# Low weight parts by an accumulating DMA, used last, in a hybrid DeltaNet, Conformer and diffusion step

## The chip, the cores and the metric

The kernel runs on one core of a Trainium2 chip. The metric is the device time of one execution in microseconds (us); lower is better. Where several runs are given, their median and their lowest and highest time stand beside each other.

## What is computed

One trunk layer on 640 tokens: 128 context tokens and 512 latent tokens, in five chunks of 128. The reference in its core:

```python
h = rmsnorm(x, norm1) * (1 + sc1) + sh1          # adaLN modulation from c @ w_ada
p = h @ w_in                                     # 1024 -> 7200 columns
qkv, z, ab, glu, gates = jnp.split(p, SPLITS, axis=-1)
qkv = silu(dwconv_seq(qkv, conv_qkv))            # width 5
o, s_fin = bidir_delta(q, k, v, g, beta, s0)     # 8 heads, both directions, chunks of 64
y_a = (rmsnorm(o, norm_o) * silu(z)) @ w_a_out
u = dwconv(glu_a * sigmoid(glu_b)) + b_dw        # width 31
y_b = silu(layernorm(u, ln_g, ln_b)) @ w_b_out
x = x + g1 * ((sigmoid(ga) * y_a + sigmoid(gb) * y_b) @ w_o)
h2 = rmsnorm(x, norm2) * (1 + sc2) + sh2
x = x + g2 * ((silu(h2 @ wg) * (h2 @ wu)) @ w_down)
```

All of it is in fp32. The matmuls multiply in a format with a shorter mantissa (fp32r in the names of tiles). A product of a weight w and an activation x is therefore made of three matmuls: each factor is split into a high part, wh and xh, which that format holds, and the low part that is left, wl = w - wh and xl = x - xh. Their sum wh·xh + wh·xl + wl·xh collects in PSUM.

## The kernel before, in words

*Stages.* Up to about 45 us the inputs and the first w_ada tiles are loaded and h is built: hh (its high part) and hl (its low part), each 8 tiles of 128 features by 640 tokens. Stage 1, 45 to 770 us, makes the 56 projections of 128 columns with w_in (`proj_in`, L448), each followed by what its columns are for: `conv_silu` (L472) for q, k and v, gates for z and for the merge, the wide convolution; beside them run the DeltaNet's decay matrices, the inverses by blocks and the scans of eight heads. At its end come half of w_a_out (`first_half`, L906) and w_b_out (`conv_branch`, L912). From L1069 on, 770 us to the end, follow the rest of w_a_out, w_o, w_gu and w_down.

*A projection.* `proj` (L131) loops over the 8 tiles of 128 rows of the weights (kt), over the three products, and over the two halves of the tokens (256 and 384 columns, `HALVES`): 48 matmuls, called a unit here. For each kt the low part of the weights is needed directly behind its two high products.

*A weight tile.* `load_w` (L117) takes the next of four buffers in rotation (`NWR` = 4, `w_slots`), lets SyncE issue the load into it (wr, L121), lets ScalarE write the high part into one of two buffers wh (L107 of `split`), and an engine subtract (L108 of `split`): wl = wr - wh. wl is the same memory as wr, read as another type. `low["eng"]` says which engine subtracts: VectorE (V) from L115 on, GpSimd (G) from L1070 on; the first two loads, `pre[1024]` and `pre[0]` (L262, L266), name VectorE themselves. `ada_part` (L460) takes the next of the same four buffers for a tile of w_ada, 32 times, so that units and w_ada tiles then alternate, and uses it in 8 small matmuls (L468) behind the unit.

*What sets the order.* The program is written by a planner, a loop (L1060) over five generators (scans, inverses, preps, gather, mains), each of which gives out a piece of the work and a cost in us; the one with the lowest sum so far is next. The order on each engine is that of the program's text as the scheduler places it; each engine takes its instructions in order, and waits on semaphores for the others. The loads stand in SyncE's queue. GpSimd makes small work in stage 1: memsets of the convolution's edges (L477), inverse square roots by a power (L521), masks (L589), the row operations of the inverses (L603), casts (L655).

*The lines of the prediction.* L478, L481 and L485 are ScalarE's copies, first tap and tanh of `conv_silu`, L483 and L487 VectorE's other taps and the last product; L494 transposes the result on TensorE for the chunks of a head. L600, L603, L609, L611, L615 and L626 are the inverses; L714 to L764 the scan, in which L740 scales v by a decay and L744 is the matmul that updates the state. aux<-atd, tgd<-tb, tb<-tgd and og<-ogd are transfers to and from scratch tensors in DRAM (atd, tgd, ogd).

Of the kernel before, what the change touches and what calls it, by code (L numbers as in the profile page):

```python
# [9 lines left out]
F32 = mybir.dt.float32  # L10
# [4 lines left out]
AF = mybir.ActivationFunctionType  # L15
ALU = mybir.AluOpType
# [3 lines left out]
P = 128  # L20
# [35 lines left out]
def hybrid_step(ctx, tc, I, O):  # L56
    nc = tc.nc
    es = ctx.enter_context
    V, S_, G, PE = nc.vector, nc.scalar, nc.gpsimd, nc.tensor
# [40 lines left out]
    def g3(ap, a):  # L100
        return ap.rearrange("p (a b) -> p a b", a=a)
# [4 lines left out]
    def split(hi, lo, x, lo_eng=None):  # L106
        S_.activation(hi, x, AF.Identity)  # L107
        return (lo_eng or V).tensor_tensor(out=lo, in0=x, in1=hi.bitcast(F32), op=ALU.subtract)  # L108
# [3 lines left out]
                          mybir.DependencyInfo(mybir.DependencyClass.NoSync, mybir.DependencyReason.DATA),  # L112
                          reason="order")

    low = {"eng": V}  # L115

    def load_w(src, lo_eng=None, after=None, wh=None):  # L117
        a, b = src.shape[1], src.shape[2]
        n = a * b
        wr, wl = next(w_next)  # L120
        ld = nc.sync.dma_start(out=g3(wr[:, :n], a), in_=src)  # L121
        if after is not None:
            order(ld, after)
        wh = T_("wh", "wh", F32R) if wh is None else wh
        split(wh[:, :n], wl[:, :n], wr[:, :n], lo_eng or low["eng"])
        return g3(wh[:, :n], a), g3(wl[:, :n], a)

    def cols_of(w, c0, n=P):
# [2 lines left out]
    def proj(w, xh, xl, nk, pp=None, hfs=(0, 1), cut=HALVES, tiled=False, rows=P):  # L131
        pp = pp or mm_pair()
        wh, wl = w
        for kt in range(nk):
            for j, (a, b) in enumerate(((wh, xh), (wh, xl), (wl, xh))):
                for hf in hfs:
                    c = cut[hf]
                    out, x = pp[hf][:rows, :c.stop - c.start], b[kt // 4]
                    if tiled:
                        out, x = g3(out, (c.stop - c.start) // P), x[:, c.start // P:c.stop // P, kt % 4, :]  # L140
                    else:
                        x = x[:, kt % 4, c]
                    PE.matmul(out, a[:, kt, :], x,  # L143
                              start=(kt == 0 and j == 0), stop=(kt == nk - 1 and j == 2))
        return pp

    def halves(pp, ap, cut=HALVES):
# [20 lines left out]
    rows = T_("dd", "rows")[:, :P]  # L168
    G.memset(rows, 0.0)
    for k, (nm, n) in enumerate((("c_ctx", 8), ("c", 8), ("norm1", 8), ("norm2", 8))):  # L170
        src = I[nm] if nm == "c_ctx" else I[nm][0]
# [96 lines left out]
    for pr in range(4):  # L268
        ws = wada[pr]
        pa = sm_ps()  # L270
        for kk in range(NK):
            for g in range(4):
                j, k = g // 2, g % 2
# [6 lines left out]
        for k in range(2):  # L280
            kt = 2 * pr + k
# [4 lines left out]
            for r, (c0, n) in enumerate(SPANS):  # L286
                v, hi, lo = (t[kt // 4][:, kt % 4, c0:c0 + n] for t in (xT, hh, hl))
                b = modB[:, kt, r:r + 1]
# [1004 lines left out]
```

## Time and profile before

| what | value |
| --- | --- |
| median of 3 runs | 1344.68 us |
| lowest and highest | 1344.32 and 1345.86 us |
| the profiled execution | 1345.78 us, its span 1342.9 us |
| granted TensorE clock, mean | 0.985 of full speed |
| ScalarE busy | 503.2 us, 37% of the span |
| VectorE busy | 842.3 us, 63% of the span |
| GpSimd busy | 298.1 us, 22% of the span |
| DMA | 157.31 MB, mean 117 GB/s |

The span is the time between the first and the last instruction that the profiler saw; the execution's own time holds 2.9 us more. Busy shares are means over stages with different limits, so the prediction reads them by stage. In a row, L143 is line 143 of the kernel before, `mm<-hh,wl` is output and inputs by their names in the program, PE is TensorE, DVE VectorE, ACT ScalarE, POOL GpSimd and SP SyncE; PEld is TensorE's loading of stationary tiles, and a q behind a name (SPq) is the queue that issues an engine's DMAs.

### The profile page before, as it was taken

The page shows a single profiled execution, that of the slowest core. Times are in us where ns is not written, and L with a number is a line of the kernel's source. Part 1 is how long each engine was busy: PE and PEld are TensorE (multiplying, and loading weights), DVE is VectorE, ACT ScalarE, POOL GpSimd, SP SyncE. Part 2 cuts the span into 40 slices and gives each one's busy share as a digit, 9 for nine tenths or more (in the row PEclk, how much of TensorE's full clock was granted, in tenths as well). Part 3 has the DMA queues.
Part 4 walks back from the last instruction along what each step waited for, and adds up shares of the span by engine and source line. Part 5 has one row for each costly group of instructions (what it writes and reads, how often), then busy time and mean ns, then how long its engine had stood idle before and what let it go on. Part 6 is the DMA issues. An engine that isn't in the chain of part 4 may idle for free.

```text
span 1342.9 us, 23244 instructions
## 1 busy us (share of the span) xinstructions
PE 1280.9 (95%) x9180; PEld 1200.7 (89%) x9180; DVE 842.3 (63%) x1663; ACT 503.2 (37%) x1080; POOL 298.1 (22%) x305
## 2 busy tenths in 40 slices
PE   5987999997999999999988999999999999999997
PEld 4986998996998999999988998899988999889996
DVE  5677896999766899998686784621224212243136
ACT  4326655343454554525354233432211222112223
POOL 1203312220010312211010036433300333003304
PEclk9988998999999999999999999999999999999999
DMA  9312443443343453324455893122222222222222
GB/s 338 114 54 83 122 150 128 127 139 91 116 123 100 140 146 98 108 78 128 138 182 191 288 288 95 51 76 79 79 77 67 78 79 79 65 77 79 79 71 86
DMA packets 179293, 157.31 MB, mean 117 GB/s; under 512 B 8032, under 2 KB 150769, under 8 KB 179185
## 3 DMA queue, kind: packets, MB, share of 16 engines
q1 hardware_dynamic: 179185, 155.83, 37.4%
q8 instruction: 72, 1.18, 0.4%
q14 instruction: 36, 0.29, 0.1%
HBM read 131.80 MB, written 24.00 MB: 116 GB/s over the span
## 4 chain that ended last, share of the span: by engine, by line
PE 58%; DVE 7%; DMA 3%; issue 2%; ACT 2%; POOL 1%; SPq 0%; POOLq 0%; DVEq 0%; ACTq 0%
PE mm L143 36%; PE sm L1113 9%; PE mm L1113 4%; PE sm L143 1%; PE sm L734 1%; PE sm L758 1%; DVE wl L108 1%; DMA aux<-atd 1%; PE sm L1158 1%; DMA og<-ogd 1%; PE sm L661 1%; PE sm L744 1%; PE sm L714 1%; POOL x L1209 1%; PE sm L494 1%
## 5 line engine op out<-in xcount | busy, mean ns | idle before, releaser
L107 ACT ACTIVATE wh<-wr 128x1024 fp32r<-128x1024 f32 (+1 forms) x154 | 152.6, 992 | 460.8 <-PE mm L143 177.3
L143 PE MATMUL mm<-hh,wh 128*128 128x384 f32 (+1 forms) x896 | 220.2, 320 | 5.5 <-ACT ci L478 3.6
L143 PE MATMUL mm<-hl,wh 128*128 128x384 f32 (+1 forms) x896 | 217.9, 316 | 0.0
L143 PE MATMUL mm<-hh,wl 128*128 128x384 f32 (+1 forms) x896 | 214.9, 315 | 0.4 <-DVE wl L108 0.4
L108 POOL TENSOR_TENSOR wl<-wr,wh 128x1024 fp32r<-128x1024 f32 (+1 forms) x59 | 132.9, 2255 | 355.6 <-ACT wh L107 343.4
L108 DVE TENSOR_TENSOR wl<-wr,wh 128x1024 fp32r<-128x1024 f32 (+1 forms) x95 | 109.0, 1148 | 104.4 <-ACT wh L107 93.1
L143 PEld LDWEIGHTS mm<-hh,wh 128*128 128x128 f32 x896 | 162.1, 191 | 12.7 <-issue 4.7
L143 PEld LDWEIGHTS mm<-hl,wh 128*128 128x128 f32 x896 | 165.6, 191 | 0.1
L143 PEld LDWEIGHTS mm<-hh,wl 128*128 128x128 f32 x896 | 164.2, 190 | 1.2 <-DVE wl L108 0.9
L143 PE MATMUL mm<-h2h,wl 128*128 128x256 f32 (+1 forms) x672 | 155.5, 309 | 0.0
L143 PE MATMUL mm<-h2l,wh 128*128 128x256 f32 (+1 forms) x672 | 154.7, 308 | 0.0
L143 PE MATMUL mm<-h2h,wh 128*128 128x256 f32 (+1 forms) x672 | 154.6, 307 | 0.0
L1259 DVE TENSOR_TENSOR ft<-ft,mm 128x256 f32<-128x256 f32 (+1 forms) x42 | 18.6, 482 | 189.4 <-PE mm L143 189.3
L143 PEld LDWEIGHTS mm<-h2h,wh 128*128 128x128 f32 x672 | 123.5, 189 | 0.2
L143 PEld LDWEIGHTS mm<-h2h,wl 128*128 128x128 f32 x672 | 122.7, 189 | 0.0
L143 PEld LDWEIGHTS mm<-h2l,wh 128*128 128x128 f32 x672 | 122.1, 188 | 0.0
L483 DVE SCALAR_TENSOR_TENSOR acc<-ci,colA,acc 128x642 f32<-128x642 f32 x96 | 86.7, 905 | 7.1 <-ACT acc L481 6.1
L1113 PE MATMUL sm<-wh,fh 128*128 128x512 f32 x152 | 60.4, 397 | 0.0
L1113 PE MATMUL sm<-wl,fh 128*128 128x512 f32 x152 | 60.0, 395 | 0.0
L1113 PE MATMUL sm<-wh,fl 128*128 128x512 f32 x152 | 59.6, 392 | 0.0
L108 DVE TENSOR_TENSOR fl<-ft,fh 128x640 fp32r<-128x640 f32 x22 | 46.5, 2112 | 16.5 <-ACT fh L107 16.5
L609 DVE TENSOR_TENSOR stmp<-M,X 128x30 f32<-128x30 f32 (+14 forms) x120 | 43.7, 364 | 3.2 <-POOL X L603 1.8
(346 smaller groups left out, 2427.2 us busy)
## 6 DMA issues: line engine op xcount, KB each, us to landing
wr<-in_w_in SPq DMA_DIRECT2D x56, 512.0 KB
wr<-in_w_gu SPq DMA_DIRECT2D x44, 512.0 KB
wr<-in_w_ada SPq DMA_DIRECT2D x32, 512.0 KB
wr<-in_w_down SPq DMA_DIRECT2D x22, 512.0 KB
wada<-in_w_ada SPq DMA_DIRECT2D x8, 1024.0 KB
atd<-et SPq DMA_DIRECT2D x40, 128.0 KB
aux<-atd SPq DMA_DIRECT2D x40, 128.0 KB
tgd<-tgt SPq DMA_DIRECT2D x16, 320.0 KB
```

Of the source, the lines that this page charges most:

```text
L107: S_.activation(hi, x, AF.Identity)
L108: return (lo_eng or V).tensor_tensor(out=lo, in0=x, in1=hi.bitcast(F32), op=ALU.subtract)
L143: PE.matmul(out, a[:, kt, :], x, start=(kt == 0 and j == 0), stop=(kt == nk - 1 and j == 2))
L483: V.scalar_tensor_tensor(out=acc[:, :n], in0=ci[:, k:k + n], scalar=vA[:, k, ct:ct + 1], in1=acc[:, :n], op0=ALU.mult, op1=ALU.add)
L494: PE.transpose(pt[:, c, :], src(c0 + c), ident)
L609: V.tensor_tensor(out=t, in0=bc(M[:, j + 1:, j:j + 1], [P, n, j]), in1=bc(X[:, j:j + 1, 0:j], [P, n, j]), op=ALU.mult)
L661: PE.matmul(pt[:, j, :], lhs[j], rhs[j], start=True, stop=True)
L714: PE.matmul(pr[:, d, j, :], TT[j].kT[:, ck[d], :], S[:, d, j, :], start=True, stop=True)
L734: PE.matmul(pv[:, d, j, :], Y1[:, d, j, ck[d], :], rhs, start=True, stop=True)
L744: PE.matmul(pS[:, d, j, :], TT[j].ktok[:, ck[d], :], vw[:, d, j, :], start=True, stop=True)
L1113: PE.matmul(acc[i], a[kt // 4][:, kt % 4, c], b[:, k2, :], start=(kt == 0 and j == 0), stop=(kt == nk - 1 and j == 2))
L1259: V.tensor_tensor(out=d, in0=d, in1=s, op=ALU.mult)
```

## The change

70 loads of weights in stage 1 are concerned: 54 tiles of 128x1024 (512 KB each) of w_in, and 16 of 128x512 (256 KB each) of w_a_out and w_b_out. For these, the low part is no longer subtracted by VectorE. ScalarE writes wh as before, then a second pass writes -wh over the loaded tile (wl and wr are one memory), and GpSimd issues a DMA that reads the same weights from DRAM again and adds them to what lies in wl: -wh + w. The two early loads keep VectorE's subtraction, and from L1070 on (L1078 of the changed kernel) the loads keep GpSimd's.

In `proj`, for every projection of the kernel, the products with wh come first, over all kt, and the products with wl follow, over all kt. The number of matmuls and what they add up stay.

```diff
--- before.py
+++ after.py
@@ -112,7 +112,7 @@
                           mybir.DependencyInfo(mybir.DependencyClass.NoSync, mybir.DependencyReason.DATA),
                           reason="order")
 
-    low = {"eng": V}
+    low = {"eng": None}
 
     def load_w(src, lo_eng=None, after=None, wh=None):
         a, b = src.shape[1], src.shape[2]
@@ -122,7 +122,13 @@
         if after is not None:
             order(ld, after)
         wh = T_("wh", "wh", F32R) if wh is None else wh
-        split(wh[:, :n], wl[:, :n], wr[:, :n], lo_eng or low["eng"])
+        if lo_eng is None and low["eng"] is None:
+
+            S_.activation(wh[:, :n], wr[:, :n], AF.Identity)
+            S_.activation(wl[:, :n], wh[:, :n].bitcast(F32), AF.Identity, scale=-1.0)
+            G.dma_start(out=g3(wl[:, :n], a), in_=src, accum_op=ALU.add)
+        else:
+            split(wh[:, :n], wl[:, :n], wr[:, :n], lo_eng or low["eng"])
         return g3(wh[:, :n], a), g3(wl[:, :n], a)
 
     def cols_of(w, c0, n=P):
@@ -131,17 +137,19 @@
     def proj(w, xh, xl, nk, pp=None, hfs=(0, 1), cut=HALVES, tiled=False, rows=P):
         pp = pp or mm_pair()
         wh, wl = w
-        for kt in range(nk):
-            for j, (a, b) in enumerate(((wh, xh), (wh, xl), (wl, xh))):
-                for hf in hfs:
-                    c = cut[hf]
-                    out, x = pp[hf][:rows, :c.stop - c.start], b[kt // 4]
-                    if tiled:
-                        out, x = g3(out, (c.stop - c.start) // P), x[:, c.start // P:c.stop // P, kt % 4, :]
-                    else:
-                        x = x[:, kt % 4, c]
-                    PE.matmul(out, a[:, kt, :], x,
-                              start=(kt == 0 and j == 0), stop=(kt == nk - 1 and j == 2))
+        three = ((wh, xh), (wh, xl), (wl, xh))
+
+        for kt, j in [(kt, j) for kt in range(nk) for j in range(2)] + [(kt, 2) for kt in range(nk)]:
+            a, b = three[j]
+            for hf in hfs:
+                c = cut[hf]
+                out, x = pp[hf][:rows, :c.stop - c.start], b[kt // 4]
+                if tiled:
+                    out, x = g3(out, (c.stop - c.start) // P), x[:, c.start // P:c.stop // P, kt % 4, :]
+                else:
+                    x = x[:, kt % 4, c]
+                PE.matmul(out, a[:, kt, :], x,
+                          start=(kt == 0 and j == 0), stop=(kt == nk - 1 and j == 2))
         return pp
 
     def halves(pp, ap, cut=HALVES):
```

Lines behind L115 have numbers higher by up to 8 in the changed kernel: its ScalarE passes are L127 and L128, its accumulating DMA L129, the matmul of `proj` L151, the taps of `conv_silu` L491.

VectorE, in the stretch between 78 and 89 us in which the exponentials of the gates (etmp) go on beside the taps of the first convolutions (acc); before:

```order
L362 TENSOR_SCALAR etmp<-tx 128x160
L363 RECIPROCAL etmp<-etmp 128x160
L108 TENSOR_TENSOR wl_60<-wr_59,wh 128x1024
L364 TENSOR_TENSOR etmp<-tx,etmp 128x160
L487 SCALAR_TENSOR_TENSOR acc<-ci,acc 128x642
L365 TENSOR_TENSOR etmp<-etmp 128x160
L367 TENSOR_SCALAR etmp<-etmp 128x160
L369 SCALAR_TENSOR_TENSOR etmp<-etmp 128x160
```

and now, from the same operation on tx:

```order
L370 TENSOR_SCALAR etmp<-tx 128x160
L371 RECIPROCAL etmp<-etmp 128x160
L491 SCALAR_TENSOR_TENSOR acc<-ci,colA,acc 128x642
L372 TENSOR_TENSOR etmp<-tx,etmp 128x160
L491 SCALAR_TENSOR_TENSOR acc<-ci,colA,acc 128x642
L373 TENSOR_TENSOR etmp<-etmp 128x160
L491 SCALAR_TENSOR_TENSOR acc<-ci,colA,acc 128x642
L375 TENSOR_SCALAR etmp<-etmp 128x160
L491 SCALAR_TENSOR_TENSOR acc<-ci,colA,acc 128x642
L377 SCALAR_TENSOR_TENSOR etmp<-etmp 128x160 x3
L495 SCALAR_TENSOR_TENSOR acc<-ci,acc 128x642
```

The subtraction between the reciprocal and the next product on etmp is gone, and taps (L483 before, L491 now) have moved up into its place; no row of wl is left on this engine in the stretch.

GpSimd, where the first head's convolutions and inverses begin (ci are the convolution's inputs, rn the norms, Bt and L_677 the matrices of an inverse); before:

```order
L594 MEMSET Cc 128x384
L521 TENSOR_TENSOR rn<-rn,mhalf 128x5 x2
L477 MEMSET ci 128x2 x6
L589 AFFINE_SELECT Bt<-Bt 128x640 x2
L477 MEMSET ci 128x2 x3
L655 TENSOR_TENSOR L_677<-Bt,off_102 128x512
L655 TENSOR_TENSOR L_680<-Bt,off_102 128x512
```

and now:

```order
L129 DMA wl_56<-in_w_in 128x8x128
L602 MEMSET Cc 128x384
L529 TENSOR_TENSOR rn<-rn,mhalf 128x5 x2
L485 MEMSET ci 128x2 x6
L129 DMA wl_60<-in_w_in 128x8x128
L597 AFFINE_SELECT Bt<-Bt 128x640 x2
L485 MEMSET ci 128x2 x3
L663 TENSOR_TENSOR L_677<-Bt,off_102 128x512
L663 TENSOR_TENSOR L_680<-Bt,off_102 128x512
L129 DMA wl_56<-in_w_in 128x8x128
```

Between the memsets, powers and masks there now stand the accumulating DMAs, three in this piece, each of which waits for ScalarE's second pass on its tile; what is written behind them in this queue comes after them.

TensorE, in a unit of the stretch in which w_ada tiles share the buffers (hh and hl are the activations, mm the PSUM tile); before, from the w_ada matmuls on:

```order
L468 MATMUL mm<-wr_57,sc 32x128 x8
L143 MATMUL mm<-hh_132,wh 128x256
L143 MATMUL mm<-hh_132,wh 128x384
L143 MATMUL mm<-hl_134,wh 128x256
L143 MATMUL mm<-hl_134,wh 128x384
L143 MATMUL mm<-hh_132,wl_60 128x256
L143 MATMUL mm<-hh_132,wl_60 128x384
```

and now, at the end of the high products:

```order
L151 MATMUL mm<-hh_133,wh 128x256
L151 MATMUL mm<-hh_133,wh 128x384
L151 MATMUL mm<-hl_135,wh 128x256
L151 MATMUL mm<-hl_135,wh 128x384
L151 MATMUL mm<-hh_132,wl_60 128x256
L151 MATMUL mm<-hh_132,wl_60 128x384
L151 MATMUL mm<-hh_132,wl_60 128x256
L151 MATMUL mm<-hh_132,wl_60 128x384
```

Before, wl follows wh by two pairs of matmuls, eight times in a unit. Now 32 matmuls on wh come first, and the 16 on wl stand together behind them.

## Rows read from the trace of the kernel before

**Rows 1.** Page, part 1: busy us (share of the span) and instructions of each engine

```profile
PE 1280.9 (95%) x9180; PEld 1200.7 (89%) x9180; DVE 842.3 (63%) x1663; ACT 503.2 (37%) x1080; POOL 298.1 (22%) x305
```

**Rows 2.** By stage: window, its length, each engine's busy us, granted clock, DMA share, GB/s

```profile
45.00:770.00 725.00, 687.28 (x5480) 650.98 (x5479) 600.57 (x1314) 336.27 (x817) 125.76 (x192) 0.98 0.42 128
770.00:1342.90 572.90, 563.25 (x3327) 522.60 (x3325) 215.22 (x280) 150.49 (x226) 165.26 (x88) 1.00 0.29 89
```

**Rows 3.** TensorE's waits, whole span: us in total, times, longest us

```profile
PE sm L494 <- ACT ci L485: 8.3, 1, 8.3
...
PE sm L744 <- DVE vw L740: 3.7, 3, 1.8
...
PE mm L143 <- ACT ci L478: 3.6, 1, 3.6
...
PE sm L661 <- ACT XA L626: 3.1, 2, 2.0
```

**Rows 4.** VectorE's groups, 45 to 770 us: busy us, mean ns; idle before

```profile
L108 DVE TENSOR_TENSOR wl<-wr,wh 128x1024 fp32r<-128x1024 f32 x54 | 67.4, 1248 | 26.8 <-ACT wh L107 26.6
...
L108 DVE TENSOR_TENSOR wl<-wr,wh 128x512 fp32r<-128x512 f32 x16 | 11.0, 688 | 1.8 <-ACT wh L107 1.6
```

**Rows 5.** ScalarE's first pass (L107): count, duration min/median/max in ns, first and last start

```profile
L107 ACT ACTIVATE wh<-wr x70: 614/1058/1104, 55.0 to 767.7; 128x1024 fp32r<-128x1024 f32 x54, 128x512 fp32r<-128x512 f32 x16
```

**Rows 6.** VectorE's time line from 72 us: start, duration, instruction [idle before]

```profile
72.70 1.23 DVE L108 TENSOR_TENSOR wl<-wr,wh 128x1024 fp32r<-128x1024 f32 x1 [1.58 <-ACT wh L107]
...
79.76 1.23 DVE L108 TENSOR_TENSOR wl<-wr,wh 128x1024 fp32r<-128x1024 f32 x1 [0.29 <-ACT wh L107]
...
86.83 1.22 DVE L108 TENSOR_TENSOR wl<-wr,wh 128x1024 fp32r<-128x1024 f32 x1
...
88.20 0.82 DVE L487 SCALAR_TENSOR_TENSOR acc<-ci,acc 128x642 f32<-128x642 f32 x1
...
106.33 1.23 DVE L108 TENSOR_TENSOR wl<-wr,wh 128x1024 fp32r<-128x1024 f32 x1 [0.79 <-ACT wh L107]
```

**Rows 7.** TensorE's time line: the ends of the two longest waits

```profile
89.56 0.58 PE L143 MATMUL mm<-hh,wh 128*128 128x256 f32 x1 [3.59 <-ACT ci L478]
...
111.20 1.30 PE L494 MATMUL sm<-ident,K 128*128 128x128 f32 x5 [8.28 <-ACT ci L485]
```

**Rows 8.** The columns of rows 2, for the stretch after the first of them

```profile
89.50:96.50 7.00, 6.95 (x36) 6.95 (x37) 1.29 (x7) 0.38 (x2) 0.44 (x2) 0.59 0.00 1
```

**Rows 9.** The DMA issues of SyncE's queue, 453 to 461 us

```profile
453.23 0.39 SPq L121 DMA_DIRECT2D wr<-in_w_in  x1
...
459.85 0.38 SPq L121 DMA_DIRECT2D wr<-in_w_in  x1
```

**Rows 10.** ScalarE's time line: the passes that these loads release

```profile
457.89 1.06 ACT L107 ACTIVATE wh<-wr 128x1024 fp32r<-128x1024 f32 x1 [0.35 <-DMA wr<-in_w_in]
...
465.68 1.04 ACT L107 ACTIVATE wh<-wr 128x1024 fp32r<-128x1024 f32 x1
```

**Rows 11.** TensorE's time line: starts of two units' w_ada matmuls

```profile
459.70 0.66 PE L468 MATMUL mm<-wr,sc 128*32 128x128 f32 x16
...
468.64 0.66 PE L468 MATMUL mm<-wr,sc 128*32 128x128 f32 x16
```

**Rows 12.** The chain of waits, 455 to 480 us: start, us, what

```profile
469.31 7.24 PE mm L143 x48
```

**Rows 13.** All matmuls on w_ada tiles: min/median/max ns, first and last start

```profile
L468 PE MATMUL mm<-wr,sc x512: 272/273/422, 100.9 to 497.8; 128*32 128x128 f32 x171
```

**Rows 14.** GpSimd's groups, 45 to 770 us (columns of rows 4)

```profile
L521 POOL TENSOR_TENSOR rn<-rn,mhalf 128x5 f32<-128x5 f32 x16 | 21.9, 1372 | 88.2 <-DVE rn L520 88.2
```

**Rows 15.** The columns of rows 2, for the end of the stage

```profile
700.00:770.00 70.00, 65.28 (x475) 64.69 (x475) 48.56 (x114) 24.66 (x60) 2.51 (x2) 0.98 0.76 245
```

**Rows 16.** The chain of waits, 700 to 780 us: its first and last transfers

```profile
706.74 6.00 DMA aux<-atd
...
774.16 4.72 DMA og<-ogd
```


## The prediction

> **What bounds the kernel now.** I read the busy times of the whole span first, then the same by stage, then what TensorE waits for, and last the time line around the longest waits.
>
> TensorE is busy for 1280.9 of the 1342.9 us of the span [rows 1]. From 770 us on it has 563.25 of 572.9 us of work [rows 2]. In that stage the weights keep their subtraction, and only the order of the matmuls changes. There is nothing to gain there and I cost it at nothing: the number of matmuls and weight loads is the same, and a low part that is used later can only be waited for less.
>
> From 45 to 770 us, where the change acts, TensorE is idle for 725 - 687.28 = 37.7 us, and VectorE is busy for 600.57 of the 725 [rows 2]. Part of that idle time hangs on VectorE: the two longest waits after the start, 8.3 us for the tanh of L485 and 3.6 us for L478, stand behind VectorE's convolution taps, and the 3.7 us of L740 and the 3.1 us of L626 behind its scan and transposes [rows 3]. So at most some 19 us of TensorE's waits can answer to a lighter VectorE, and the kernel stays bound by TensorE.
>
> **The change part by part.** I sum against the profiled execution (1345.78 us; its span is 1342.9). It is 1.1 us over the median of the runs shown, so the sum, as a difference, is then taken off the median, 1344.68.
>
> *VectorE loses 70 subtractions.* 54 of 128x1024 and 16 of 128x512, 67.4 + 11.0 = 78.4 us, 13% of its work in the stage [rows 2, 4]. What of it lies on the path:
> - Before the 3.59 us wait at 89.56, the L487 that TensorE's wait goes back to starts at 88.20, and three subtractions of 1.23, 1.23 and 1.22 us stand before it, from 72.70 on [rows 6, 7]. Without them it comes up to 3.7 us earlier and the wait goes. After the wait TensorE runs from 89.5 to 96.5 at a granted clock of 0.59, mostly its 1.2 GHz level [rows 8]; at 2.4 GHz these 7 us would be 7 x 0.59 = 4.1. Together 3.6 + 2.9 = 6.5 us. But ScalarE now has a second pass for each tile, and one of 1.06 us [rows 5] may stand before L485 or L478. Then a wait of 1 us stays and some of the slow clock with it. I take -4.5, with bounds 0 and -6.5.
> - In the 8.28 us wait that ends at 111.20, the subtraction at 106.33 stands between the taps, 1.23 us after 0.79 us in which VectorE waited for ScalarE [rows 6, 7]. I take -2.0. The taps themselves, late next, keep the other 6.3 us.
> - In the other waits on VectorE, the 6.8 us of L740 and L626 [rows 3] and smaller ones, some 10 us, the queue ahead is 13% shorter: -1.3, rounded up to -1.5; bounds 0 and -5.
>
> *ScalarE gains 70 passes.* At the measured 1058 ns and 614 ns that is 54 x 1.06 + 16 x 0.61 = 67 us [rows 5], and its busy share of the stage goes from 336.27/725 = 46% to 56% [rows 2]. A wait of TensorE on ScalarE meets a new pass in about one case in ten: +1.0, bounds 0 and +4.
>
> *The accumulating transfer replaces the subtraction.* No row shows one, so I bound its time X from GpSimd's issue to landing. Below, a plain load of the same 512 KB: issued at 453.23, it let ScalarE start at 457.89, 4.66 us. The next one took 459.85 to 465.68, 5.83 us [rows 9, 10]. Above, twice the last figure and 1 us, 12.7 us, since it has to read the tile as well as the weights. I take 7.0, half as much again as 4.66, because only the reading is doubled.
> What covers it is the unit of 48 matmuls. In the units that share their four buffers with w_ada, every second unit has the same buffer. The tightest pitch is 459.70 to 468.64, 8.94 us [rows 11], and the low parts are now the last third of a unit's 7.24 us, 2.41 [rows 12]. From the last use of a buffer to the first use of its new low part there are 2 x 8.94 - 2.41 = 15.5 us. The reload takes 0.15 for the issue, 5.83 for the load and 2 x 1.06 on ScalarE, 8.1 us, and leaves 7.4 us for X. At the mean pitch of these 32 units, (497.8 - 100.9)/31 = 12.8 us [rows 13], it leaves 15.1. So X = 7.0 just fits: +0.5, for what is tighter than I see.
> The Trainium skill ("DMA: Bandwidth & Descriptors", Anatomy of one DMA) gives such a transfer 2.0 us and its bytes at 436 GB/s, an estimate of 3.2 us here; the plain load already took 4.66 us, so the measurement decides, and by the page this term would be 0.
>
> *The DMA engines carry more.* 54 x 512 KB + 16 x 256 KB = 32 MB are read a second time. In most of the stage they are under half busy. From 700 to 770 us they are 76% busy at 245 GB/s [rows 15], and five transfers on the chain of waits, 25 us together, lie between 706 and 779 [rows 16]. The 16 small tiles bring 4.2 MB there, 13 us at 245/0.76 = 322 GB/s, so the share goes to some 90%. If the chain's transfers stretch by 8%, that is +2.0; bounds 0 and +4.5 (18%, as the share).
>
> *GpSimd issues the 70 transfers in its own queue.* Each waits there for ScalarE's second pass, with convolution memsets, powers and masks queued behind it. GpSimd has 125.76 us of work in the 725 [rows 2], so it has room, but no row has the price of one issue: SP's are 0.38 us [rows 9], and at 9.7 us each (the other 599 us over 54 large and 16/2 small ones) the queue would be full. I take a value near SP's, under 2 us, since that is the nearest row: +0.5, bounds 0 and the third rival.
>
> Sum: -4.5 - 2.0 - 1.5 + 1.0 + 0.5 + 2.0 + 0.5 = -4.0 us, or 1344.68 - 4.0 = **1340.7 us**. If the gains all come at their bounds and the costs at none, it is -13.5, 1331.
>
> **The rivals.**
> 1. *No change* (1344.7, within 2.7 us, that is 0.2%, about what a measurement of this kernel tells from none). TensorE's later waits take back what the early ones give: the taps behind the 8.28 us wait are a chain of their own, and a new place on TensorE's queue waits instead. For it speaks that TensorE is 95% busy in the stage, against it that both long waits show the subtraction in the chain. Chance 0.17.
> 2. *The low part lands late, slower.* The place is the dense run of units from 440 to 500 us. With X = 12.7 two units take 0.15 + 5.83 + 2.12 + 12.7 + 2.41 = 23.2 us in place of 17.9, 2.65 us more for each of some 7 units: +18.5, so -4.5 + 18.5 = +14, 1359 us. It decides from the X at which 7 units lose the 4 us gained, about 7.4 + 2 x 4/7 = 8.5 us. For it: the gap of 7.4 is barely above 7.0. Against it: elsewhere the pitch leaves twice that. Chance 0.21. The Trainium skill ("Collectives: The Full Stack", The bandwidth ceiling) says that an add in the DMA engines reads two sources by two descriptors per chunk; no row here shows an add, and by that rule X lies at the upper end.
> 3. *GpSimd becomes the late engine, slower.* At 5 us an issue it is busy for 126 + 62 x 5 = 436 of 725 us, and an operation of it waits behind an issue for 0.43 x 2.5 = 1.1 us on average. Some 12 of its steps follow each other in each of four head pairs (the power of 1.37 us [rows 14] is one): 51 us of chain. If TensorE lacks cover for a quarter, +13, less the 4: +9, 1354 us. Chance 0.12. The Trainium skill ("SBUF — State Buffer", SBUF: two separate sides) warns of just this: GpSimd cannot write descriptors while VectorE holds the shared port in a two-port mode; no run here shows such a transfer yet.
> 4. *More than forecast*: the waits of L740 and L626 go as well, 4.5 + 2.0 + 6.8 = 13.3 of gain less the 4.0 of costs: 1335.4 us. Chance 0.05.
>
> **How the numbers follow.** The forecast has 0.45. Faster by over 0.2% are the forecast and rival 4, 0.45 + 0.05 = 0.50; within it rival 1, 0.17; slower rivals 2 and 3, 0.33. The likeliest case alone spans 1336 to 1342. The range goes from 1331, the sum of the gains, to 1359, rival 2's bound, and leaves some 0.15 beyond, most of it above.
>
> **What would show it.** Right: TensorE's two waits near 86 and 103 us shortened, VectorE near 520 us busy between 45 and 770, ScalarE near 400, no wait of L151 on a DMA of wl worth over 1 us in total, the stage after 770 as long as before. Wrong: L151 waiting on wl in the units near 440 to 500 (rival 2); GpSimd's queue long at L129 with waits of TensorE or VectorE on its powers, masks and casts (rival 3); the waits moved to other lines at the same total (rival 1).

## The result, and the profile after

The changed kernel takes 1355.57 us (median of 9 runs, 1350.3 to 1361.36) against 1344.17 for the kernel before beside it (9 runs, 1341.04 to 1345.86): the ratio is 1.0088, 95% interval 1.0065 to 1.0111. It is slower, by some 11 us, where 4 us less were forecast. The profiled execution is the median one; its span is 1353.9 us. Page, part 1, of the changed kernel, as [rows 1]:

```profile
PE 1277.9 (94%) x9180; PEld 1196.7 (88%) x9180; DVE 754.9 (56%) x1593; ACT 566.1 (42%) x1150; POOL 402.5 (30%) x375
```

The same by stage, as [rows 2]:

```profile
45.00:770.00 725.00, 676.98 (x5418) 639.11 (x5416) 534.68 (x1226) 392.89 (x881) 221.78 (x258) 0.98 0.76 167
770.00:1353.90 583.90, 572.37 (x3399) 532.61 (x3399) 193.06 (x294) 156.84 (x232) 172.76 (x92) 0.99 0.31 95
```

VectorE has less to do in stage 1 (600.57 to 534.68 us), and TensorE has got less done there all the same (687.28 to 676.98). The column that jumps is the last but one: the DMA engines' share rises from 0.42 to 0.76, for bytes that rise by 30% (128 to 167 GB/s). What TensorE waits for (columns of [rows 3]):

```profile
PE mm L151 <- DMA wl<-in_w_in: 6.0, 4, 2.9
PE mm L151 <- issue: 5.9, 2, 4.6
...
PE mm L151 <- DVE tb L977: 4.0, 3, 3.0
...
PE mm L151 <- DMA wl<-in_w_b_out: 1.6, 2, 1.1
```

The 8.3 and 3.6 us of [rows 3] are gone, as forecast. In their place stand waits on the low part from the DMA, and on tb (L977), which itself waits for transfers.

### The profile page after: what moved, and what is told of

Read it like the earlier page. It is cut to its first block, busy times and chain, and to the rows that moved or that the text cites. A ratio compares the mean times of both kernels' runs of the same rounds, so it can differ in the third digit from the quotient of the medians.

```text
span 1353.9 us, 23435 instructions
## 1 busy us (share of the span) xinstructions
PE 1277.9 (94%) x9180; PEld 1196.7 (88%) x9180; DVE 754.9 (56%) x1593; ACT 566.1 (42%) x1150; POOL 402.5 (30%) x375
## 3 DMA queue, kind: packets, MB, share of 16 engines
q0 software_dynamic: 64608, 32.51, 19.7%
## 4 chain that ended last, share of the span: by engine, by line
PE 67%; DMA 11%; DVE 11%; ACT 4%; issue 3%; SPq 1%; POOL 1%; POOLq 0%; ACTq 0%; DVEq 0%
PE mm L151 42%; PE sm L1121 9%; PE mm L1121 4%; DMA wr<-in_w_in 3%; PE sm L669 2%; PE sm L151 2%; DMA wl<-in_w_in 2%; DMA tgd<-tb 2%; DMA atd<-et 1%; DVE uacc L856 1%; PE mm L476 1%; DVE uacc L853 1%; DVE X L619 1%; DVE stmp L617 1%; ACT XA L634 1%
## 5 line engine op out<-in xcount | busy, mean ns | idle before, releaser
L151 PE MATMUL mm<-hh,wh 128*128 128x384 f32 (+1 forms) x896 | 219.7, 320 | 4.9 <-ACT wh L127 3.7
L151 PE MATMUL mm<-hl,wh 128*128 128x384 f32 (+1 forms) x896 | 211.8, 313 | 0.2 <-DVE hl L300 0.2
L107 ACT ACTIVATE wh<-wr 128x1024 fp32r<-128x1024 f32 (+1 forms) x84 | 85.5, 1020 | 294.8 <-PE mm L1121 97.9
L151 PEld LDWEIGHTS mm<-hh,wh 128*128 128x128 f32 x896 | 160.9, 189 | 11.6 <-issue 4.7
L151 PE MATMUL mm<-hh,wl 128*128 128x256 f32 (+1 forms) x896 | 155.4, 320 | 10.6 <-DMA wl<-in_w_in 6.0
L151 PEld LDWEIGHTS mm<-hl,wh 128*128 128x128 f32 x896 | 163.4, 189 | 0.7 <-DVE hl L300 0.5
L129 POOL DMA_DIRECT2D wl<-in_w_in x54 | 85.2, 1577 | 235.7 <-ACT wl L128 114.6
L151 PE MATMUL mm<-h2l,wh 128*128 128x256 f32 (+1 forms) x672 | 153.1, 307 | 0.0
L151 PE MATMUL mm<-h2h,wh 128*128 128x256 f32 (+1 forms) x672 | 152.9, 307 | 0.0
L151 PEld LDWEIGHTS mm<-hh,wl 128*128 128x128 f32 x896 | 139.1, 193 | 12.0 <-DMA wl<-in_w_in 7.1
L151 PEld LDWEIGHTS mm<-h2h,wh 128*128 128x128 f32 x672 | 121.8, 188 | 0.2
L151 PEld LDWEIGHTS mm<-h2l,wh 128*128 128x128 f32 x672 | 121.9, 187 | 0.0
L127 ACT ACTIVATE wh<-wr 128x1024 fp32r<-128x1024 f32 (+1 forms) x70 | 67.4, 962 | 101.8 <-DMA wr<-in_w_in 46.5
L151 PE MATMUL mm<-h2h,wl 128*128 128x256 f32 (+1 forms) x672 | 104.5, 307 | 0.0
L151 PEld LDWEIGHTS mm<-h2h,wl 128*128 128x128 f32 x672 | 100.5, 188 | 0.0
L491 DVE SCALAR_TENSOR_TENSOR acc<-ci,colA,acc 128x642 f32<-128x642 f32 x96 | 88.2, 919 | 19.8 <-ACT acc L489 18.7
L108 DVE TENSOR_TENSOR wl<-wr,wh 128x1024 fp32r<-128x1024 f32 x25 | 30.6, 1224 | 89.7 <-ACT wh L107 89.7
L128 ACT ACTIVATE wl<-wh 128x1024 fp32r<-128x1024 f32 (+1 forms) x70 | 67.3, 961 | 1.3
```

Of the source, the lines that this page charges most:

```text
L127: S_.activation(wh[:, :n], wr[:, :n], AF.Identity)
L128: S_.activation(wl[:, :n], wh[:, :n].bitcast(F32), AF.Identity, scale=-1.0)
L129: G.dma_start(out=g3(wl[:, :n], a), in_=src, accum_op=ALU.add)
L151: PE.matmul(out, a[:, kt, :], x, start=(kt == 0 and j == 0), stop=(kt == nk - 1 and j == 2))
L491: V.scalar_tensor_tensor(out=acc[:, :n], in0=ci[:, k:k + n], scalar=vA[:, k, ct:ct + 1], in1=acc[:, :n], op0=ALU.mult, op1=ALU.add)
```

## Where the time went along the span

Start times of the same instruction in two time lines show who leads where. The table gives them as differences from the kernel before, for the first scan step (L740, 278.86 us in the kernel before), the last w_ada matmuls (L468, 497.36), the first matmul behind stage 1 (L1113, 806.63) and the end of the span (1342.9). The medians and ratios of all runs stand beside them; each ratio is to the kernel before in runs on the same chip.

| kernel | median us | ratio (95% interval) | 279 | 497 | 807 | end |
| --- | --- | --- | --- | --- | --- | --- |
| the change | 1355.57 | 1.0088 (1.0065, 1.0111) | -11.2 | +0.2 | +14.3 | +11.0 |
| e1 order alone | 1352.1 | 1.0074 (1.0049, 1.0099) | -2.5 | -1.5 | +10.0 | +6.9 |
| e2 no transfer | 1314.08 | 0.9794 (0.9766, 0.9823) | -16.8 | -15.4 | -26.2 | -27.8 |
| e3 old order, adds | 1431.75 | 1.0664 (1.0618, 1.0710) | -0.3 | +39.6 | +78.1 | +78.1 |
| e4 small tiles on VectorE | 1344.06 | 1.0009 (0.9987, 1.0031) | -10.6 | +6.5 | +1.8 | -1.5 |
| e5 plain load | 1334.68 | 0.9925 (0.9897, 0.9953) | -18.9 | -14.9 | -15.0 | -18.3 |
| e8 an eighth of the add | 1320.81 | 0.9825 (0.9802, 0.9847) | -15.8 | -15.5 | -20.9 | -24.2 |
| e6 GpSimd subtracts | 1389.3 | 1.0333 (1.0307, 1.0359) | +8.5 | +22.5 | +48.9 | +45.5 |
| e9 old order, no transfer | 1321.79 | 0.9832 (0.9810, 0.9854) | -16.8 | -13.1 | -22.9 | -22.0 |
| e7 five early adds | 1343.54 | 1.0001 (0.9987, 1.0014) | -11.6 | -9.7 | +2.4 | -0.9 |
| e10 dense units on VectorE | 1344.73 | 1.0006 (0.9993, 1.0018) | -11.2 | -8.1 | +4.1 | +1.2 |
| e11 every second tile | 1325.61 | 0.9869 (0.9851, 0.9888) | -12.2 | -8.3 | -14.2 | -17.6 |
| e14 order only from 770 us | 1341.75 | 0.9988 (0.9973, 1.0003) | -3.1 | -0.6 | +0.2 | -3.1 |
| e12 early adds, order by source | 1331.42 | 0.9912 (0.9890, 0.9933) | -12.9 | -9.8 | -9.8 | -13.0 |
| e13 every second, order by source | 1337.22 | 0.9953 (0.9938, 0.9969) | -3.5 | -4.4 | -5.8 | -9.0 |
| e15 the other half | 1345.65 | 1.0017 (0.9999, 1.0035) | -7.1 | +4.3 | +6.9 | +3.5 |

e2, e5, e8 and e9 leave out or falsify low parts, so they price a piece and are no kernels to use.

The first row tells the story: 11 us ahead at 279 us, level at 497, 14 behind at 807, and 3 regained later. The forecast gain came, and two stretches took it back, the dense run of units with w_ada tiles and the end of stage 1.

Each row of differences comes from one profiled execution, and two pairs show how far such rows can be trusted. Set instruction against instruction, the changed kernel and e4 do the same work in the same order on every engine up to 673 us, and yet stand 6.3 us apart at 497. The kernel before and e14 do so up to 770 us, and stand 3.1, 0.6 and 0.2 us apart. So a few us in one column are no result by themselves. The profile of e5 is of its fastest run, 8 us under its median, and that of e3 is 9 us under its own.

## The experiments

The diffs are against the changed kernel unless another is named.

### Which part of the change costs: e1 to e4

e1, the order of the matmuls alone:

```diff
-    low = {"eng": None}
+    low = {"eng": V}
```

> The new order of the matmuls alone; the low parts are subtracted on VectorE as before. Theory A (the accumulating transfers cost what was lost; the order costs nothing, and the last 540 us, in which the changed kernel regained 4 us, owe that to the order): about 1341 us, 3 to 4 us under the kernel before, all of it after 800 us. Rival C (the order itself is what loses, as TensorE and the other engines are placed differently in stage 1): 1350 us or more.

e2, without the transfer:

```diff
-            G.dma_start(out=g3(wl[:, :n], a), in_=src, accum_op=ALU.add)
```

> The changed kernel without the accumulating transfer: ScalarE writes wh and -wh, and nothing is added (so this leaves out the low parts of 70 weight tiles). Theory A: the lead of some 12 us that the changed kernel has from 110 to 430 us stays to the end and the later stage adds 4: 1327 to 1333 us. Rival D (ScalarE's second pass takes back the gain of VectorE): 1340 us or more. What lies between this run and the changed kernel is the price of the transfers and of GpSimd's issues together.

e3, with the loop of the kernel before in `proj`:

```diff
-        for kt, j in [(kt, j) for kt in range(nk) for j in range(2)] + [(kt, 2) for kt in range(nk)]:
-            a, b = three[j]
+        for kt in range(nk):
+            for j, (a, b) in enumerate(((wh, xh), (wh, xl), (wl, xh))):
```

> The accumulating transfers as in the change, with the old order of the matmuls, so that the low part is needed behind the first two products of each kt. Theory A (the transfer lies on the way from a buffer's release to its next use): a unit's first low product comes up to 4.5 us earlier, and where the reload is tight that much is lost again; 1365 to 1395 us. Rival B (GpSimd's issues delay its other work, the landing is covered): within 5 us of the changed kernel, 1351 to 1361.

e4, only the 54 tiles of w_in by adds:

```diff
-proj(load_w(cols_of(wao[:512], 128 * m)), oh, ol, 4)
+proj(load_w(cols_of(wao[:512], 128 * m), lo_eng=V), oh, ol, 4)
-proj(load_w(cols_of(wbo, 128 * m)), sh, sl, 4)
+proj(load_w(cols_of(wbo, 128 * m), lo_eng=V), sh, sl, 4)
```

> The change for the 54 tiles of w_in alone; the 16 small tiles of w_a_out and w_b_out are subtracted on VectorE as before. Theory A: between 700 and 800 us the changed kernel fell back by some 10 us behind longer transfers (tgd<-tb up to 11.7 us) and low parts; without 4.2 MB of adds there 6 to 9 us come back: 1347 to 1350 us. Rival (the fall there is only the earlier delay carried on, or the order): 1354 to 1357.

e2 is the sharpest. Without the transfer, and with ScalarE's second pass, the kernel is 28 us faster than before. So rival D falls: the second pass is cheap. What lies between e2 and the change is 1355.6 - 1314.1 = 41.5 us. That is the transfers with their issues, and with them another placement: from 124 us on, the scheduler puts VectorE's, ScalarE's and TensorE's instructions in another order in e2 than in the changed kernel. What this is worth alone was not tried, and e1 will show that an order can be worth 10 us. e3 fits theory A's mechanism, and goes beyond its bound (1395): without the late use of the low parts, TensorE waits for them again and again. The first two lines are its counterparts of the 6.0 and 5.9 us above:

```profile
PE mm L149 <- DMA wl<-in_w_in: 39.3, 16, 6.8
PE mm L149 <- issue: 11.4, 5, 4.8
PE mm L149 <- DMA wl<-in_w_b_out: 9.3, 2, 6.5
...
PE mm L149 <- DMA wl<-in_w_a_out: 6.4, 2, 5.2
```

e4 gains 11.5 us on the change, more than expected. It stands at +6.5 at the last w_ada matmuls and at +1.8 behind stage 1: the 6.5 lie in the stretch where e4 and the change do the same work, so the distance there is spread between runs. What e4 has over the change it gets at the end of the stage, where in the changed kernel one tgd<-tb takes 11.68 us on the chain of waits (5.72 in the kernel before, at 755.05 on its chain, within the stretch of [rows 16]):

```profile
762.76 11.68 DMA tgd<-tb
```

e1 went against theory A. The order alone is 9.5 us slower, not 3 to 4 faster; all of it between 497 and 807 us (-1.5 to +10.0). That opened a question of its own, taken up by e9, e12 and e14.

### What in the transfer costs: e5, e8, e6, e9

e5, a plain load of the same bytes from the same queue, and e8, the add on an eighth of the tile:

```diff
-            G.dma_start(out=g3(wl[:, :n], a), in_=src, accum_op=ALU.add)
+            G.dma_start(out=g3(wl[:, :n], a), in_=src)
```

```diff
-            G.dma_start(out=g3(wl[:, :n], a), in_=src, accum_op=ALU.add)
+            G.dma_start(out=g3(wl[:, :n], a)[:, :1, :], in_=src[:, :1, :], accum_op=ALU.add)
```

> The changed kernel with a plain load in place of the accumulating one (the same bytes from the same queue; the low part is then the weight itself, not what the high part leaves). Between the changed kernel (1355.6) and the one without a transfer (1314.1) lie 41 us. Theory A2 (the add holds the DMA engines longer than a load: 8.2 us of 16 engines per MB against 3.2): the plain load costs about 3.2/8.2 of it, 1325 to 1337 us. Rival B2 (the issue on GpSimd and the fixed part of a landing are the price): 1348 us or more.

> The changed kernel, but the accumulating transfer covers only the first 128 of a tile's rows (an eighth of a w_in tile, a quarter of a small one; the other low parts are left out). Issue, semaphore and the fixed part of the landing stay, the bytes go. Theory A2: 1315 to 1324 us. Rival B2: 1340 us or more.

Both times lie in theory A2's ranges. The price of 41.5 us falls into three: 6.7 from 1314.1 to 1320.8 for issue, landing and the first eighth (a quarter of a small tile), 13.9 from there to 1334.7 for the bytes of a plain load, and 20.9 to 1355.6 for adding instead of loading. By the ratios, each to the kernel before on its own chip, the three are 4.2, 13.4 and 21.9. (e5's runs lie between 1326.3 and 1335.6, so the line between the last two can shift by several us.)

Only the last step is clean. In e5, TensorE, VectorE, ScalarE and SyncE run the same instructions in the same order as in the changed kernel, and GpSimd's differ in the kind of the transfer alone. This step by itself is more than the 11 us that the change lost. e8 and e2 are placed in another order from 124 us on, so the first two steps hold what that is worth, too.

Part 3 of the page shows one thing in which an add differs: packets, MB, and the time that the packets took as a share of 16 engines. First the change:

```profile
q1 hardware_dynamic: 179185, 155.83, 36.9%
q0 software_dynamic: 64608, 32.51, 19.7%
```

and e5, with plain loads on GpSimd's queue (q0):

```profile
q1 hardware_dynamic: 179185, 155.83, 38.3%
q0 software_dynamic: 64608, 32.51, 14.1%
```

Per MB the adds hold all 16 engines for 0.197 x 1353.9 / 32.51 = 8.2 us, the plain loads of that queue for 5.7, and all of SyncE's transfers for 3.2 on average. So 30% more bytes nearly double the DMA share. But this share does not price the step. From 45 to 770 us it is 0.50 in e8, 0.70 in e5 and 0.76 in the change (e5's row, columns of [rows 2]):

```profile
45.00:770.00 725.00, 694.45 (x5567) 659.11 (x5565) 547.25 (x1256) 400.08 (x891) 185.32 (x262) 0.99 0.70 178
```

Theory A2 gave a plain load 3.2 us per MB. With the 5.7 measured, its own rule makes 1314.1 + 41.5 x 5.7/8.2 = 1343 us of e5, over all five of its runs; that its range held is luck. An add of 512 KB also lands later (7.0 us against 4.9 at the median) and takes longer to issue (1.58 us against 0.90). How the 20.9 us divide among engine time, landing and issue was not tried.

e6, GpSimd as the subtracting engine, without any transfer or second pass:

```diff
-    low = {"eng": None}
+    low = {"eng": G}
```

> No accumulating transfer and one pass on ScalarE: GpSimd subtracts the 70 low parts, with the new order of the matmuls. Theory A2 (VectorE's relief is worth some 28 us with this order, and the DMA is what ate it): GpSimd's pass of 2.27 us lands sooner than the add's 7.0 and leaves the DMA engines alone, 1318 to 1332 us, under both kernels. Rival B3 (GpSimd with 130 us more of work delays its powers, masks and casts, on which the inverses and scans hang): 1345 us or more.

It is the slowest but one, as rival B3 had it and against theory A2, and not by GpSimd's queue alone. VectorE's own work became slower; its convolution taps, first in the kernel before and then in e6 (columns of [rows 4]):

```profile
L483 DVE SCALAR_TENSOR_TENSOR acc<-ci,colA,acc 128x642 f32<-128x642 f32 x96 | 86.7, 905 | 7.1 <-ACT acc L481 6.1
```

```profile
L491 DVE SCALAR_TENSOR_TENSOR acc<-ci,colA,acc 128x642 f32<-128x642 f32 x96 | 107.1, 1117 | 14.8 <-ACT acc L489 13.9
```

e9, e3 without its transfer:

> ScalarE's two passes, no transfer (low parts of 70 tiles left out), and the old order of the matmuls. Against the same with the new order (1314.1) it shows what the order does where VectorE is relieved. Theory C2 (the order costs some 9 us in stage 1 whatever makes the low parts, as it did with VectorE's subtraction): 1303 to 1308 us. Rival (the order's cost there hangs on VectorE's subtractions, and the order is worth 3 to 4 us later): 1314 to 1322 us.

1321.8 us, within the rival's range. Without transfers the new order is worth 7.7 us (1321.8 to 1314.1; 5 by the ratios), with VectorE's subtraction it costs 9.5. And the relief of VectorE, in the old order, is worth 22 us, ScalarE's second pass and the placement that goes with it included.

### Which tiles: e7, e10, e11, e15

e7 takes the adds for the five tiles ahead of the first w_ada tile alone, e10 (from e4) all w_in tiles but the last eight with w_ada, e11 (from e4) every second w_in tile, and e15 the other half of them:

```diff
 if ada_todo and len(units) > ADA_FROM:
+    low["eng"] = V
     ada_part(pp[1])
```

```diff
+low["eng"] = V if 0 < len(ada_todo) <= 8 else None
 w = pre.pop(col, None) or load_w(cols_of(w_in, col), after=after)
```

```diff
+low["eng"] = V if len(units) % 2 else None
 w = pre.pop(col, None) or load_w(cols_of(w_in, col), after=after)
```

```diff
+low["eng"] = None if len(units) % 2 else V
 w = pre.pop(col, None) or load_w(cols_of(w_in, col), after=after)
```

> New order; accumulating transfers for the first five w_in tiles alone, up to the first w_ada tile (97 us), VectorE's subtraction for all later ones. Theory A3 (the early gain, some 8 us by 130 us beyond what the order alone has, comes from these few tiles and stays, and after that the kernel goes as the order alone does, 1352): 1342 to 1346 us. Rival (without relief behind 130 us the lead is lost to VectorE, as TensorE only meets it later): 1350 to 1354 us.

> As with the 16 small tiles on VectorE (1344.1), and VectorE's subtraction too for the eight units that end the stretch with w_ada tiles, about 420 to 500 us, where that run fell from 10 us ahead to 6 us behind in waits for low parts. Theory A: most of these 16 us stay, 1330 to 1336 us, under both kernels. Rival (VectorE's eight subtractions there, or the later waits, take them back): 1341 to 1346 us.

> Accumulating transfers for every second w_in tile, VectorE for the others and for the 16 small tiles; new order. Theory A2 (the price is DMA time and the tight reload, the gain VectorE's time): half the adds cost less than half, half the relief brings about half; 1335 to 1345 us. Rival (each add on a tight buffer delays TensorE whatever stands beside it): no better than with all of them, 1344 to 1350 us.

> As the alternating run (1325.6), the other half of the w_in tiles by accumulating transfers. If its gain is one of load (half of VectorE's subtractions gone, half of the adds' DMA time) it is within 5 us of it, 1321 to 1331 us. If it was the luck of one placement: 1335 us or more.

e7: five adds give the whole early lead (-11.6 at 279, -9.7 at 497), and the end of stage 1 takes it as in e1. e10 keeps -8.1 at 497 where the change has +0.2 and e4 +6.5, as theory A says, and still ends where e4 does, as its rival says: between 497 and 807 it loses 12.2, in waits on scan steps and on tb and oh. The lead that the dense units cost can be had back, but it did not reach the end.

e11 is the fastest kernel of the study that computes everything, 18 us under the kernel before and 30 under the change, and 9 under the range expected of it. Its waits on low parts from the DMA come to 0.2 us. e15, with as many adds, is 20 us slower and no better than the kernel before. By e15's expectation that makes e11's gain the luck of one placement; two of e15's waits of TensorE:

```profile
PE mm L151 <- DMA wl<-in_w_in: 4.3, 3, 2.0
...
PE mm L151 <- issue: 3.9, 1, 3.9
```

The larger ones end at 434, 455 and 498 us, in the units 31, 33 and 37 (counted from 0). e4's largest are in the same three units, the changed kernel's in 31, 33 and 38. e11 gives 31, 33 and 37 to VectorE. So up to 497 us (-8.3 against +4.3, 12.6 us) it matters which tiles are added: the waits of 1.99, 3.86 and 1.95 us on these three make 7.8 of it. For the rest, and for 9 us between 497 and 807, the runs show no cause; e15's load is the same, so load alone is not the rule.

### The order of the matmuls: e14, e12, e13

Here `load_w` notes where its low part comes from, and `proj` uses it last only behind an add and from 770 us on. The same edit is made to e1 (e14), e7 (e12) and e11 (e13):

```diff
+            low["last"] = True
         else:
+            low["last"] = low["eng"] is G
...
-        for kt, j in [(kt, j) for kt in range(nk) for j in range(2)] + [(kt, 2) for kt in range(nk)]:
+        steps = [(kt, j) for kt in range(nk) for j in range(3)]
+        if low.get("last"):
+            steps.sort(key=lambda t: t[1] == 2)
+        for kt, j in steps:
```

> VectorE's subtraction everywhere in stage 1 with the old order of the matmuls there, the new order from 770 us on alone. Theory C3 (the order alone costs 12 to 13 us in stage 1, where VectorE subtracts, and gives 3 to 4 us back later): 1339.5 to 1341.5 us. Rival (the order's later gain is only what the tail of stage 1 leaves undone): 1343 to 1345 us.

> Five accumulating transfers up to the first w_ada tile, as in the run with the early tiles alone; the order low parts last only for those five and from 770 us on, the old order for every tile that VectorE subtracts. Theory C3: the 10 us of lead at 130 us stay through stage 1, and 3 to 4 us come later, 1329 to 1333 us. Rival (the loss between 500 and 800 us there is VectorE's load, not the order): 1341 to 1345 us.

> Every second w_in tile by an accumulating transfer with low parts last, the others by VectorE in the old order (also the 16 small ones). Theory C3: the order costs where VectorE subtracts, so this is faster than alternating with one order for all (1325.6): 1316 to 1323 us. Rival (with half the load off VectorE the order costs nothing any more): 1324 to 1329 us.

e14 and e12 bear out theory C3 in place and, within a few us, in size: with the old order in stage 1 nothing is lost between 497 and 807 (+0.8 and 0.0, where e1 loses 11.5 and e7 12.1), and 3.3 us come behind it. (These 3.3 stand in the traces, within half a us in every one with the new order there but e2. By the runs e14 is not clear of no change: 0.9988, up to 1.0003.) e12 keeps the early lead to the end, 1331.4. Where e7 loses it shows in the windows 740 to 760 and 760 to 780 us (columns of [rows 2]), first e7, then e12:

```profile
740.00:760.00 20.00, 20.00 (x151) 20.00 (x150) 13.05 (x32) 4.77 (x10) 0.00 (x0) 1.00 0.64 193
760.00:780.00 20.00, 13.10 (x77) 11.72 (x75) 13.88 (x26) 6.69 (x22) 4.49 (x3) 0.84 0.75 259
```

```profile
740.00:760.00 20.00, 19.94 (x140) 19.47 (x139) 12.61 (x26) 7.19 (x24) 1.96 (x1) 1.00 0.94 310
760.00:780.00 20.00, 17.45 (x116) 16.46 (x115) 13.65 (x27) 6.40 (x10) 5.59 (x5) 1.00 0.86 278
```

In e7 TensorE is idle for 6.9 of the last 20 us and goes on at a lower granted clock (0.84, between its levels of 1.2 and 2.4 GHz). On e7's chain of waits the last head's output then comes through VectorE's steps and two transfers:

```profile
763.80 4.67 DMA ta<-tgd
...
776.20 3.38 DMA og<-ogd
```

But e13 is slower than e11 by 12 us, against both theories. "The order costs where VectorE subtracts" is thus no rule. Each order gives another placement of the scans among the projections. That some leave TensorE work for the end of the stage and others don't fits the windows of e7 and e12, but was not tried by itself; why stays open.

## Why the prediction was wrong, step by step

**What bounds the kernel.** This held in the main. At most 19 us of TensorE's waits were said to answer to VectorE: without transfers its idle time between 45 and 800 us falls from 39.3 to 18.9 us, summed over its time line (e2). e2 gains more than these 20 us, 28: with fewer waits the granted clock from 45 to 770 us is 1.00 of 2.4 GHz, where it was 0.98. The sum had one stretch of 7 us of that.

**VectorE loses 70 subtractions: -8.0, too small.** The places were right: both long waits are gone. In the old order the relief gave 22 us (e9), with ScalarE's passes inside, for which +1.0 was taken, and with another placement. Beside the waits that I read there were those that I did not: most of the rest comes between 497 and 807 us, where e9 gains a further 9.8 us.

**The accumulating transfer: +0.5, the step that failed.** X itself was right at the median; the issues of L129 for w_in in the changed kernel, and the landings of all 70:

```profile
L129 POOL DMA_DIRECT2D wl<-in_w_in x54: 1527/1561/1802, 56.4 to 661.4; - x54
...
DMA to landing us min/median/max: 4.5/7.0/11.5
```

The median is the 7.0 that I took, for the 54 of 512 KB alone (6.1 to 11.3) as for all. What failed is its cover, "X = 7.0 just fits", for which I set one X against a gap of 15.5 us. One tight place, in the changed kernel's time lines of SyncE, ScalarE, GpSimd and TensorE:

```profile
434.47 0.37 SPq L121 DMA_DIRECT2D wr<-in_w_in  x1
...
438.71 1.06 ACT L127 ACTIVATE wh<-wr 128x1024 fp32r<-128x1024 f32 x1 [1.89 <-DMA wr<-in_w_in]
439.80 1.06 ACT L128 ACTIVATE wl<-wh 128x1024 fp32r<-128x1024 f32 x1
...
441.36 1.63 POOL L129 DMA_DIRECT2D wl<-in_w_in  x1 [4.04 <-ACT ci L486]
...
431.86 2.59 PE L151 MATMUL mm<-hh,wl 128*128 128x256 f32 x16 [1.84 <-DMA wl<-in_w_in]
...
451.75 2.15 PE L151 MATMUL mm<-hh,wl 128*128 128x256 f32 x7 [4.62 <-issue]
```

The buffer is released at 434.45, when the 16 low products from 431.86 end. The low products that need it again stand ready at 451.75 - 4.62 = 447.13: a gap of 12.7 us, not 15.5, as the w_ada matmuls (L476) of these two units start 7.2 us apart, at 434.37 and 441.58, not 8.94. The reload takes 4.2 us for the load, 2.2 on ScalarE and 0.5 until GpSimd issues, which leaves 5.8 us for X. The profile calls what ended the wait "issue", but the landing of this one add tells:

```profile
DMA to landing us min/median/max: 10.3/10.3/10.3
```

Issued at 441.36 it lands 10.3 us later, at 451.7, and the matmuls start at 451.75. Even the median of 7.0 would not have fitted there, and the tail of X met the shortest gap. Rival 2 had the place (three units there, not seven) but tied it to an X of 8.5 throughout. Up to 497 us the waits on low parts are 1.84, 4.62 and 0.30 us, 6.8 of the 11.4 lost from 279 on; one of 2.95 follows at 506.59. Most of the rest is no price of the add: e5, with the same order of work, loses 4.0 us on that stretch, too.

By the Trainium skill ("DMA: Bandwidth & Descriptors", Anatomy of one DMA) X would have been an estimated 3.2 us. The fastest add of 512 KB took 6.1, and e5's plain loads of that size 4.3 to 8.6, so by the measurement the page's sum is too low here, beside DMA engines that are 70 to 76% busy.

**The DMA engines carry more: +2.0, bounded by +4.5, mis-sized most.** I counted bytes, and for the end of the stage alone. Adding in place of loading costs 20.9 us in the same order of work (e5 to the change); bytes and adds together 34.8 (e8 to the change, with another placement), over both stretches. From 497 to 807 the change loses 14.1 us, e5 with plain loads nothing in its trace (it gains 0.1; this is its fastest run), and e2 gains 10.8. The row for it did not exist before; rows for the nearest transfers gave time by byte, and the adds hold the engines 2.6 times as long per MB as SyncE's transfers do. The share was mis-added besides: 13 us of 70 on top of 0.76 are 0.95, not some 0.90; the changed kernel shows 0.87 from 700 to 770 us. How much of the 20.9 us is engine time, and how much the later landing priced above, stays open. The Trainium skill ("Collectives: The Full Stack", The bandwidth ceiling) has a reason ready: in a ReduceScatter the add needs two source reads. The trace agrees in direction, with 8.2 against 5.7 us per MB on one queue, a ratio of 1.4. I had used that rule for the latency X, and not for the engines' time.

**GpSimd issues: +0.5.** An issue for a w_in tile takes 1.58 us on average, within the 2 us that I allowed, and all 70 take 107 us. In e8 one takes 0.88, and with landing and the first bytes they cost 6.7 us; what the longer issue of a full add costs more is part of the 20.9 us and was not tried by itself. Rival 3, at 5 us an issue, did not come; that its 1354 us lies beside the measured 1355.6 is chance.

**The order: nothing, "can only be waited for less".** It was not nothing anywhere. With the adds it saves 76 us (e3), without any transfer 7.7 (e9 to e2), from 807 us on 3.3 in the traces, and with VectorE's subtraction it costs 9.5 (e1). That a product waits less says nothing of the order in which the scheduler then places everything else.

## What to carry to other kernels

Price a transfer twice: by its latency against the tightest gap of the buffer that it fills, and by the time that it holds the DMA engines, which other transfers on the path then lack; an add in flight is dearer than its bytes (20.9 us over a plain load in the same order of work). Where work is moved from a full engine to a resource with little slack, try parts of it: here five tiles held the whole early gain, and all of them lost 11 us. Which part counts as much as how much: one half of the w_in tiles gained 18 us, the other half nothing. And an order of instructions is a change of its own, to be tested alone.

## What the runs showed that was not expected

A subtraction on VectorE that starts while one runs on GpSimd ends only behind it. Behind 770 us this happened to the splits of the FFN activations (fl) in the kernel before, e3 and e9, which have the old order there, and not in the change, e1, e2, e11 and e14, which have the new one. The kernel before, then the changed kernel:

```profile
L108 DVE TENSOR_TENSOR fl<-ft,fh 128x640 fp32r<-128x640 f32 x22 | 46.5, 2112 | 16.5 <-ACT fh L107 16.5
```

```profile
L108 DVE TENSOR_TENSOR fl<-ft,fh 128x640 fp32r<-128x640 f32 x22 | 19.9, 905 | 19.1 <-ACT fh L107 19.1
```

In the kernel before, one that starts at 942.86 beside GpSimd's pass (942.17 to 944.56) takes 2.38 us and ends at 945.24, 0.7 us behind that pass; one without such a neighbour takes 0.82. The Trainium skill ("SBUF — State Buffer", SBUF: two separate sides) calls the port pair that the two engines share an exclusive lock, taken by a VectorE operation with two inputs in SBUF against a GpSimd operation that reads SBUF; these rows and e6's taps (905 to 1117 ns) agree. What rival 3 feared, an issue held up by VectorE, shows once in the changed kernel. The issues of w_in tiles take at most 1.80 us, but one of a small tile takes 2.27, against a median of 1.30 for w_a_out, and ends just behind an operation of VectorE:

```profile
774.33 2.27 POOL L129 DMA_DIRECT2D wl<-in_w_a_out  x1 [0.89 <-ACT wl L128]
```

```profile
775.15 1.22 DVE L1101 TENSOR_SCALAR g1b<-g1b 128x2048 f32<-128x2048 f32 x1
```

Beside the same operation the longest small issue of e5 (1.59 us, median 0.76) and of e8 (1.38, median 0.88) stand, too. It is about 1 us for one issue of 70, far from rival 3's price. Whether the shorter subtractions are the 3.3 us regained behind 807 us was not tried.
